# Non-weight transfers issued by GpSimd in a hybrid decoder kernel, with a changed table chain

## The chip, the cores and the metric

One core of one Trainium2 chip. The time is device microseconds of one execution of the program, the median of the runs shown. Engines are called as in the profile: PE (TensorE), DVE (VectorE), ACT (ScalarE), POOL (GpSimd) and SP (SyncE, which here only issues transfers).

## The reference, cut to what matters

Two layers of a decoder trunk, on 512 prompt tokens and 8 sample tokens together (520 columns), width 1024, FFN width 2816, all in fp32.

```python
def decoder_layer(x, ...):
    h = rms_norm(x, norm_g[0])
    x = x + 0.5 * rms_norm(swiglu(h, ...ffn 0), norm_g[1])
    h = rms_norm(x, norm_g[2])
    xq, xf, xi, xg, gu, gv, su, gate_cols = split(h @ w_in)
    a_out, s_hg_new = hgrn2_mixer(xq, xf, xi, xg, s_hg, lb, hgrn_norm_g)
    b_out, v_rows = gmlp_mixer(gu, gv, ...)
    c_out, h_re_new, h_im_new = s5_mixer(su, h_re, h_im, lam, log_dt, b, c, d, glu_w, glu_b)
    merged = sum(sigmoid(gates) * (branches @ w_branch))
    x = x + rms_norm(merged @ w_out, norm_g[3])
    h = rms_norm(x, norm_g[4])
    return x + 0.5 * rms_norm(swiglu(h, ...ffn 1), norm_g[5]), states
```

The S5 mixer is a complex diagonal recurrence, with `abar = exp(lam * dt)` and input and output matrices built from powers of abar. The kernel builds those matrices itself, as 16 tables (8 per layer).

## The kernel before, in words

Columns are held in two halves of 256 and 264. Every product is made of three matmuls (`mm3`: L122 weight high part by activation high part, L123 weight low part by activation high part, L125 weight high part by activation low part). A weight tile of 128x1024 is loaded by SP into `raw` (L102), ACT makes the high part `whi` (L103), DVE subtracts and makes the low part `wlo` (L107); with `share` the subtraction is done by POOL instead, in `ptt` (L237). `share` is asked for in two pairs of the first part of an FFN and in `ffn_units`, 25 tiles in all.

An FFN runs in three parts (`FF_PARTS`: 7, 7, 8 blocks of 128). Each part has up products (two matmul groups, `scaled` into `va` and `vb` on DVE, L129, silu on ACT, product on DVE, L416, then the split into `hid`, L115 on ACT and L116) and then down products over 8 output blocks.

Side work is cut into generators and advanced by `tick(us)`: each tick adds us over the step's price to a counter, and the generator goes on by one yield for each whole unit. `s5_tables` is such a generator in the first FFN, with the price `STEP_P`. It loads constants, computes the HGRN lower bounds (L516 to L531), then the S5 parameters (`s5_params`, from L569: dt = e^log_dt at L582 on POOL, xr = lam_r * dt at L585 on DVE, powers, sines and cosines, complex products in `cmul`, L504 to L509), and then the 16 tables (`s5_table`). A table takes POOL 19 instructions: `er` and `ei` (L665 to L667), `tb` 3 (L683 to L688), `cmul` for the next `bar` and a memset of `tb` 2 (L674). PE multiplies `er` and `ei` by `rc` (L695) into `tb` 0 and, through ACT copies (L704) and DVE (L709), into `tb` 2. Then four stores put `tb` 0 to 3 into memory (L711). `er` and `ei` exist once, so those of the next table can only be written when L695 has read the last ones. The FFN's last part begins after `before_last`, which drains what is left of the generator.

In the mixer, the S5 scan is another such generator, next to the HGRN heads and the gMLP. Its input is turned over through memory: `ud` and `us` are stored (L771, L772) and loaded back as `ub`, which lies in the `y` tiles (L777, L779). For each of 8 steps it loads four tables (L795), PE projects (L803), POOL saves and replaces columns of `w` (L827 to L830), DVE scans, and PE multiplies by the tables (L857 to L859). Every second step's result goes through memory once more (`zd`, L867 and L870).

At a block boundary (`residual`) x is updated, its high part `h` is made by ACT (`pre_hi`), its low part by DVE (`pre_lo`), squares are summed, and `norm_rows` has PE reduce the sum (`mean_w`, L257). DVE makes the inverse root there (`rs_s`, L225 to L233) and a diagonal matrix (`diag`, L268 and L272), and PE spreads it over the partitions (L279). The first norm of the program sums the squares one tile at a time (`sq_sum`, L218).

All 920 transfers are issued by SP, in program order, and each waits there for its data and its room. Every engine runs its own instructions in a fixed order.

Of the kernel before, what the change touches and what calls it, by code (L numbers as in the profile page):

```python
# [9 lines left out]
F32 = mybir.dt.float32  # L10
# [23 lines left out]
STEP_P, STEP_S, STEP_H = 3.9, 2.0, 3.1  # L34
# [11 lines left out]
class Trunk:  # L46
# [29 lines left out]
    def load_consts(self):  # L76
        nc, t, c = self.nc, self.t, self.const
        self.mask = c.tile([P, 64 + 3 * SEGS * 32], U8, name="mask")
        with self.tc.tile_pool(name="mkp", bufs=1) as pool:
            m = pool.tile([P, 64 + 3 * SEGS * 32], F32, name="m")  # L80
            nc.sync.dma_start(m, t["level_mask"])
            nc.gpsimd.tensor_copy(self.mask, m)
        self.tri = c.tile([P, P], F32, name="tri")
        nc.sync.dma_start(self.tri, t["tri_mask"])
        self.hg = c.tile([P, DEPTH * 4], F32, name="hg")
        nc.sync.dma_start(self.hg, t["hgrn_norm_g"])
        self.glub = c.tile([P, DEPTH * 8], F32, name="glub")
        nc.sync.dma_start(self.glub, t["glu_b"])
# [6 lines left out]
    def unit(self, src, *shape, pool=None, share=False):  # L95

        nc = self.nc
        n = math.prod(shape)
        raw = self.wp.tile([P, 1024], F32, tag="raw", name="raw", bufs=RAW_BUFS)
        hi = (pool or self.wp).tile([P, 1024], F32R, tag="whi", name="whi")  # L100
        lo = (pool or self.wp).tile([P, 1024], F32R, tag="wlo", name="wlo")
        nc.sync.dma_start(raw[:, :n], src)  # L102
        nc.scalar.copy(hi[:, :n], raw[:, :n])  # L103
        if share:
            self.ptt(lo[:, :n], raw[:, :n], hi[:, :n].bitcast(F32), ALU.subtract)
        else:
            nc.vector.tensor_tensor(lo[:, :n], raw[:, :n], hi[:, :n].bitcast(F32), ALU.subtract)  # L107
        pat = {2: "p (a b) -> p a b", 3: "p (a b c) -> p a b c"}[len(shape)]
        kw = dict(zip("abc", shape))
        return hi[:, :n].rearrange(pat, **kw), lo[:, :n].rearrange(pat, **kw)  # L110
# [232 lines left out]
    def residual(self, half, r1, y2, x2, pre, spill):  # L343
        nc, v, sl, w = self.nc, self.nc.vector, SL[half], HW[half]
        if pre is not None and half == 0:
            self.new_h()
        acc = self.acc2_room()[:, :, :w] if pre is not None else None
        for q in range(KD // 2):
            t, xs = y2[q][:, :, sl], x2[q][:, :, sl]
            v.tensor_tensor(t, t, r1[:, None].to_broadcast([P, 2, w]), ALU.mult)  # L350
            v.tensor_tensor(xs, t, xs, ALU.add)
            for e in range(2):
                j = 2 * q + e
                if pre is None:
                    nc.sync.dma_start(self.t["y"][j][:, sl], xs[:, e])
                    continue
                self.pre_hi(*pre, half, j)
                if spill is not None:
                    nc.sync.dma_start(spill[j][:, sl], xs[:, e])
            if pre is not None:  # L360
                yield
        if pre is None:
            return
        for q in range(KD // 2):
            xs = x2[q][:, :, sl]
            self.pre_lo(*pre, half, 2 * q)
            self.pre_lo(*pre, half, 2 * q + 1)
            if q == 0:
                nc.scalar.activation(acc, xs, AF.Square)
                continue  # L370
            t = y2[q][:, :, sl]
            nc.scalar.activation(t, xs, AF.Square)
            if q == 1:
                v.scalar_tensor_tensor(acc, t, 4e-6, acc, ALU.add, ALU.add)
            else:
                v.tensor_tensor(acc, acc, t, ALU.add)
            if q == 1:
                yield
        self.h_done[half] = True
        yield  # L380
        v.tensor_tensor(acc[:, 0], acc[:, 0], acc[:, 1], ALU.add)
        self.norm_rows(acc[:, 0], half)

    def sq_sum(self, acc, xs):

        for j, x in enumerate(xs):
            self.sq_acc(acc, x, j)
# [10 lines left out]
    def ffn(self, l, f, hid_pool, gain, finish, lo_eng=None, first=(), before_last=None, ahead=()):  # L398
# [3 lines left out]
        for part, nk in enumerate(FF_PARTS):  # L402
            hid = [hid_pool.tile([P, 2, NT], F32R, tag="hid", name="hid") for _ in range(nk)]

            def up(mi, half, u):
                (gh, gl), (uh, ul) = u
                pg, pu = self.pst(half), self.pst(half)
                xs = self.hx(half)
                self.mm3(pg, [(gh[:, k], gl[:, k]) for k in range(KD)], xs)
                self.passed()  # L410
                self.mm3(pu, [(uh[:, k], ul[:, k]) for k in range(KD)], xs)
                a, b, s = self.tmph("va", half), self.tmph("vb", half), self.tmph("sil", half)
                self.scaled(a, pg, half)
                nc.scalar.activation(s, a, AF.Silu)  # L414
                self.scaled(b, pu, half)
                nc.vector.tensor_tensor(b, b, s, ALU.mult)  # L416
                self.split(hid[mi][:, :, SL[half]], b, lo_eng)
                if m0 + mi >= 2:
                    self.tick(5.2)

            def pair(m, pool=None):
                share = part == 0 and LEAD <= m < LEAD + 2
                return [self.take(lambda: self.unit(t["w_up"][l, f, m0 + m, :, k], 8, 128, pool=pool, share=share))
                        for k in range(2)]
# [86 lines left out]
    def lower_bounds(self):  # L511

        nc, c = self.nc, self.const
        with self.tc.tile_pool(name="lbp", bufs=1) as pool:
            z = pool.tile([P, DEPTH, 4], F32, name="lb_z")
            nc.sync.dma_start(z, self.t["lb_logits"])  # L516
# [16 lines left out]
    def s5_tables(self, pool):  # L533
# [13 lines left out]
        def load(i):  # L547
            bc = pool.tile([P, 4, 2, 32], F32, tag="bc", name="bc", bufs=3)
            nc.sync.dma_start(bc, self.t["s5_bc"][i // 8, i % 8])
            return bc  # L550
# [18 lines left out]
    def s5_params(self, pool, NPR, k):  # L569
# [5 lines left out]
        nc.sync.dma_start(lr, t["lam_re"])  # L575
        nc.sync.dma_start(li, t["lam_im"])
        nc.sync.dma_start(ld, t["log_dt"])
        nc.sync.dma_start(k["d"], t["s5_d"])
# [27 lines left out]
        for i in range(3):  # L606
            self.cmul(pool, ar, ai, fr[:, :, i], fi[:, :, i], fr[:, :, i + 1], fi[:, :, i + 1], [NPR], v, "cs")
        v.memset(er[:, :, 3], 1.0)
# [32 lines left out]
    def s5_table(self, pool, l, s, k, rc, bc):  # L641
# [68 lines left out]
        for i in range(4):  # L710
            nc.sync.dma_start(dst[i], tb[i])  # L711
# [11 lines left out]
    def proj_block(self, l, m, evac, share=False):  # L723
        self.pu = self.unit(self.t["w_in"][l, m], 8, 128, share=share)
        for half in (0, 1):
            self.proj(l, m, half, lambda p: evac(half, p))
        self.tick(5.3)
# [4 lines left out]
    def ffn_units(self, l, f):  # L732
        return [lambda i=i: self.unit(self.t["w_up"][l, f, i // 2, :, i % 2], 8, 128, share=i % 2 == 0) for i in range(5)]

    def s5_project(self, l, f_block, ev_f):
# [32 lines left out]
        for m in range(4):  # L768
            d = self.dr.tile([P, 4, NT // 4], F32, tag="ud", name="ud", bufs=4)
            ds = self.dr.tile([P, NS], F32, tag="us", name="us", bufs=4)  # L770
            nc.sync.dma_start(d, ups[m])  # L771
            nc.sync.dma_start(ds, uss[m])  # L772
# [3 lines left out]
            for j in range(4):  # L776
                nc.sync.dma_start(ub[32 * j:32 * j + 32, :, :128], dv[j][:, :, :128])  # L777
            for j, c in ((3, 128), (0, 136)):
                nc.sync.dma_start(ub[32 * j:32 * j + 32, :, c:c + NS], ds.rearrange("(q c) n -> c q n", q=4))  # L779

    def s5_scan(self, l, pool):
# [5 lines left out]
        nc.sync.dma_start(st, t["state_s5"][l])  # L787
# [4 lines left out]
        def table(i, s, bufs=1):  # L792
            x = self.tab[l * n + s][i]
            tb = pool.tile([int(d) for d in x.shape], F32, tag=f"tab{i}", name="tab", bufs=bufs)
            nc.sync.dma_start(tb, x)  # L795
# [18 lines left out]
        for s in range(n):  # L814
# [50 lines left out]
            if lp == 2:  # L865
                d = self.dr.tile([P, 4 * NB], F32, tag="zd", name="zd", bufs=4)
                nc.sync.dma_start(d, zb.rearrange("p q n -> p (q n)"))  # L867
                dv = d.rearrange("(j c) (q n) -> q c j n", j=4, q=4)
                for k in range(4):
                    nc.sync.dma_start(zz[32 * k:32 * k + 32], dv[k])  # L870
# [18 lines left out]
        nc.sync.dma_start(t["s5_sample"][l], new)  # L889
        nc.sync.dma_start(t["s5_prompt"][l], fin)  # L890
# [55 lines left out]
    def tok_proj(self, name, l, c, evac, share=False):  # L946

        nc = self.nc
        us = [self.unit(self.t[name][l, c, kk], 4, 256, share=share) for kk in range(2)]
# [34 lines left out]
    def hgrn_values(self, l, hh, pool, V):  # L984
# [13 lines left out]
        nc.sync.dma_start(vd, vs)  # L998
# [36 lines left out]
    def hgrn_head(self, l, h, V, q0, qs, k, f, sg, pool, last):  # L1035
# [80 lines left out]
        def load(b0):  # L1116
            st = pool.tile([P, 2, P], F32, tag="st", name="st", bufs=2)
            nc.sync.dma_start(st, t["state_hgrn"][l, h][:, b0:b0 + 2])
            vb = pool.tile([P, 2, P], F32, tag="vb", name="vb", bufs=2)
            for b in range(2):  # L1120
                nc.sync.dma_start(vb[:, b], vd[b0 + b].partition_broadcast(P))
            loaded.append((st, vb))

        def state(b0):
# [4 lines left out]
            nc.sync.dma_start(t["hgrn_sample"][l, h][:, b0:b0 + 2], st)  # L1129
# [56 lines left out]
        nc.sync.dma_start(t["hgrn_prompt"][l, h], S[3])  # L1186
# [41 lines left out]
    def gmlp_norm(self, l, pool):  # L1228
# [3 lines left out]
        nc.sync.dma_start(ng, t["gmlp_ng"][l])  # L1232
        nc.sync.dma_start(nb, t["gmlp_nb"][l])
# [18 lines left out]
        nc.sync.dma_start(t["gmlp_v"][l], vt[4][:NS])  # L1252

    def gmlp_mix(self, l, pool, fill):
# [4 lines left out]
        nc.sync.dma_start(ws, t["gmlp_ws"][l])  # L1259
        bs = pool.tile([P, 4, P], F32, name="bs")  # L1260
        nc.sync.dma_start(bs, t["gmlp_bs"][l])
        w00 = pool.tile([NS, 4], F32, name="w00")
        nc.sync.dma_start(w00, t["gmlp_w00"][l])
# [31 lines left out]
    def mixer(self, l, xd, finish, ahead):  # L1295
# [46 lines left out]
        with tc.tile_pool(name=f"mh{l}", bufs=KD) as mh:  # L1342
# [4 lines left out]
            for j in range(KD):  # L1347
                nc.sync.dma_start(self.x[j], xd[j])
# [17 lines left out]
    def run(self, ctx):  # L1366
# [7 lines left out]
        def start(half):  # L1374
# [3 lines left out]
            self.sq_sum(accs[half], [self.x[j][:, SL[half]] for j in range(KD)])  # L1378
# [144 lines left out]
```

## Time and profile before

| | us |
|---|---|
| median of 3 runs (2705.0 to 2705.9) | 2705.61 |
| the profiled execution | 2704.64 |
| its span, first to last instruction | 2702.8 |
| PE busy | 2640.5 (98%) |
| DVE busy | 1597.4 (59%) |
| ACT busy | 1062.8 (39%) |
| POOL busy | 573.1 (21%) |

The span lies within the profiled execution; 1.8 us are around it. Mean granted clock of PE over the span is 0.993. Issuing a transfer doesn't count as busy, on any engine. Waits are given as the idle time of an engine ahead of an instruction, with the instruction that ended it last.

### The profile page before, as it was taken

What the parts mean: (1) busy time and instruction counts of PE and PEld (TensorE: products, weight loads), DVE (VectorE), ACT (ScalarE), POOL (GpSimd) and SP (SyncE); (2) the same over time, 40 slices, a digit from 0 to 9 for tenths busy, and PEclk for the clock granted to TensorE, in tenths of its full rate; (3) what the DMA queues carried; (4) which work ended last, traced back from release to release, by engine and by line L of the source; (5) the groups of instructions that cost most, each with busy time, mean ns of one, the idle gap of its engine ahead of it and who ended that gap; (6) DMA issues with size and microseconds to landing.
All of it is one profiled execution on the core that took longest, in us unless ns stands there. A gap on an engine that the chain in (4) does not pass through costs nothing.

```text
span 2702.8 us, 53557 instructions
## 1 busy us (share of the span) xinstructions
PE 2640.5 (98%) x21600; PEld 2615.5 (97%) x21600; DVE 1597.4 (59%) x3421; ACT 1062.8 (39%) x2166; POOL 573.1 (21%) x772
## 2 busy tenths in 40 slices
PE   8899999999999999999999999999999999999998
PEld 7899999999999999999999999998999999999998
DVE  8567877886675473344473344679866545534444
ACT  4244454453333453322443323544434335433232
POOL 5478920220021122011121101012100111201010
PEclk9999999999999999999999999999999999999999
DMA  4344453553232413322322232355332233232331
GB/s 140 102 137 150 151 159 113 171 159 96 88 95 87 141 56 95 97 91 95 94 79 87 93 96 89 123 152 169 116 99 90 89 107 111 69 98 88 99 94 48
DMA packets 131704, 291.22 MB, mean 108 GB/s; under 512 B 19024, under 2 KB 59632, under 8 KB 131456
## 3 DMA queue, kind: packets, MB, share of 16 engines
q1 hardware_dynamic: 131456, 287.79, 33.5%
q8 instruction: 170, 2.79, 0.4%
q14 instruction: 78, 0.64, 0.1%
HBM read 257.07 MB, written 30.67 MB: 106 GB/s over the span
## 4 chain that ended last, share of the span: by engine, by line
PE 80%; issue 7%; DVE 6%; POOL 4%; DMA 2%; ACT 1%; SPq 0%; DVEq 0%; POOLq 0%; ACTq 0%
PE mm L122 24%; PE mm L125 24%; PE mm L123 24%; PE mm L956 1%; PE mm L958 1%; PE mm L957 1%; DMA raw<-in_w_in 1%; PE aux L1073 1%; PE aux L279 1%; PE aux L257 1%; PE aux L695 0%; DVE h L317 0%; DVE acc L218 0%; PE aux L803 0%; DMA x<-in_xT 0%
## 5 line engine op out<-in xcount | busy, mean ns | idle before, releaser
L122 PE MATMUL mm<-h,whi 128*128 128x256 f32 (+1 forms) x4224 | 1059.0, 287 | 22.5 <-ACT h L313 7.0
L123 PE MATMUL mm<-h,wlo 128*128 128x256 f32 (+1 forms) x4224 | 1047.8, 284 | 1.9 <-DVE wlo L107 1.9
L122 PEld LDWEIGHTS mm<-h,whi 128*128 128x128 f32 x4224 | 799.8, 189 | 25.5 <-issue 8.2
L123 PEld LDWEIGHTS mm<-h,wlo 128*128 128x128 f32 x4224 | 802.2, 190 | 3.8 <-DVE wlo L107 3.0
L103 ACT CAST whi<-raw 128x1024 fp32r<-128x1024 f32 (+1 forms) x424 | 437.5, 1032 | 515.6 <-PE mm L125 431.4
L107 DVE TENSOR_TENSOR wlo<-raw,whi 128x1024 fp32r<-128x1024 f32 (+1 forms) x399 | 486.7, 1220 | 243.8 <-ACT whi L103 240.1
L125 PE MATMUL mm<-h,whi 128*128 128x256 f32 (+1 forms) x4224 | 596.9, 284 | 0.0
L125 PEld LDWEIGHTS mm<-h,whi 128*128 128x128 f32 x4224 | 544.4, 189 | 0.1
L122 PE MATMUL mm<-hid,whi 128*128 128x256 f32 (+1 forms) x1408 | 349.6, 285 | 3.6 <-ACT hid L115 3.6
L123 PE MATMUL mm<-hid,wlo 128*128 128x256 f32 (+1 forms) x1408 | 347.8, 283 | 0.0
L116 POOL TENSOR_TENSOR hid<-vb,hid 128x256 fp32r<-128x256 f32 (+1 forms) x132 | 132.5, 1004 | 871.8 <-ACT hid L115 858.9
L129 DVE TENSOR_TENSOR va<-mm,r 128x256 f32<-128x256 f32 (+1 forms) x320 | 136.0, 425 | 279.9 <-PE mm L125 274.9
L122 PEld LDWEIGHTS mm<-hid,whi 128*128 128x128 f32 x1408 | 265.8, 189 | 3.9 <-ACT hid L115 3.8
L123 PEld LDWEIGHTS mm<-hid,wlo 128*128 128x128 f32 x1408 | 266.3, 189 | 0.1
L125 PE MATMUL mm<-hid,whi 128*128 128x256 f32 (+1 forms) x1408 | 201.0, 283 | 0.0
L129 DVE TENSOR_TENSOR vb<-mm,r 128x256 f32<-128x256 f32 (+1 forms) x176 | 74.9, 425 | 188.6 <-PE mm L125 188.5
L125 PEld LDWEIGHTS mm<-hid,whi 128*128 128x128 f32 x1408 | 183.0, 189 | 0.0
L115 ACT CAST hid<-vb 128x256 fp32r<-128x256 f32 (+1 forms) x176 | 72.1, 410 | 277.5 <-DVE vb L416 274.2
L414 ACT ACTIVATE sil<-va 128x256 f32<-128x256 f32 (+1 forms) x176 | 73.7, 419 | 148.0 <-DVE va L129 142.1
L447 DVE TENSOR_TENSOR y<-mm,y 128x264 f32<-128x264 f32 (+1 forms) x128 | 54.3, 426 | 112.9 <-PE mm L125 112.3
L416 DVE TENSOR_TENSOR vb<-vb,sil 128x256 f32<-128x256 f32 (+1 forms) x176 | 84.1, 478 | 16.5 <-ACT sil L414 2.5
L958 PE MATMUL mm<-whi,h 128*128 128x256 f32 (+1 forms) x320 | 90.5, 283 | 0.0
(445 smaller groups left out, 3600.5 us busy)
## 6 DMA issues: line engine op xcount, KB each, us to landing
raw<-in_w_up SPq DMA_DIRECT2D x176, 512.0 KB, 3.6
raw<-in_w_in SPq DMA_DIRECT2D x88, 512.0 KB, 3.6
raw<-in_w_down SPq DMA_DIRECT2D x64, 448.0 KB, 3.3
raw<-in_w_down SPq DMA_DIRECT2D x32, 512.0 KB, 3.4
tab<-tb SPq DMA_DIRECT2D x48, 256.0 KB, 2.4
tab<-tab SPq DMA_DIRECT2D x48, 256.0 KB, 2.9
raw<-in_w_branch SPq DMA_DIRECT2D x24, 512.0 KB, 4.0
raw<-in_w_out SPq DMA_DIRECT2D x16, 512.0 KB, 4.0
```

The lines of the kernel that those rows point to most:

```text
L103: nc.scalar.copy(hi[:, :n], raw[:, :n])
L107: nc.vector.tensor_tensor(lo[:, :n], raw[:, :n], hi[:, :n].bitcast(F32), ALU.subtract)
L115: nc.scalar.copy(pair[:, 0], src)
L116: (lo_eng or nc.gpsimd).tensor_tensor(pair[:, 1], src, pair[:, 0].bitcast(F32), ALU.subtract)
L122: mm(out, wh, x[:, 0], start=first and k == 0, stop=False)
L123: mm(out, wl, x[:, 0], start=False, stop=False)
L125: mm(out, wh, x[:, 1], start=False, stop=last and k == n - 1)
L129: self.nc.vector.tensor_tensor(dst, p, self.rms(half), ALU.mult)
L414: nc.scalar.activation(s, a, AF.Silu)
L416: nc.vector.tensor_tensor(b, b, s, ALU.mult)
L447: nc.vector.tensor_tensor(ys, pd, ys, ALU.add)
L958: nc.tensor.matmul(p, self.h[k][:, 1, tk], wh, start=False, stop=k == KD - 1)
```

## The change

Four parts.

1. Every transfer but weights, the x input, norm_g and the result y is issued by GpSimd (`nc.gpsimd.dma_start` for `nc.sync.dma_start`). SP keeps 457 transfers, POOL gets 463. Among them, over the program: table stores 64, table loads 64, `vb` 64, `st` 32, hgrn states out 32, `ub` 48, `zz` 32, `xd` stores 32 and loads 16, `bc` 16, `ud`, `us` and `zd` 8 each.
2. `share` is gone: DVE makes every `wlo`.
3. In `residual` the squares and their sums move into the loop behind `pre_hi`, and all `pre_lo` come behind; `norm_rows` follows without a yield of its own. `sq_sum` takes two tiles at a time.
4. `STEP_P` 3.9 becomes 3.2, the generator is ticked in the first FFN's up blocks from the fifth on rather than the third, and `s5_params` has a yield more in a loop of three complex products.

```diff
-STEP_P, STEP_S, STEP_H = 3.9, 2.0, 3.1
+STEP_P, STEP_S, STEP_H = 3.2, 2.0, 3.1
...
-        if share:
-            self.ptt(lo[:, :n], raw[:, :n], hi[:, :n].bitcast(F32), ALU.subtract)
-        else:
-            nc.vector.tensor_tensor(lo[:, :n], raw[:, :n], hi[:, :n].bitcast(F32), ALU.subtract)
+        nc.vector.tensor_tensor(lo[:, :n], raw[:, :n], hi[:, :n].bitcast(F32), ALU.subtract)
...
                 if spill is not None:
-                    nc.sync.dma_start(spill[j][:, sl], xs[:, e])
-            if pre is not None:
-                yield
+                    nc.gpsimd.dma_start(spill[j][:, sl], xs[:, e])
+            if pre is None:
+                continue
+            nc.scalar.activation(acc if q == 0 else t, xs, AF.Square)
+            if q == 1:
+                v.scalar_tensor_tensor(acc, t, 4e-6, acc, ALU.add, ALU.add)
+            elif q:
+                v.tensor_tensor(acc, acc, t, ALU.add)
+            yield
         if pre is None:
             return
...
+        v.tensor_tensor(acc[:, 0], acc[:, 0], acc[:, 1], ALU.add)
+        for j in range(KD):
+            self.pre_lo(*pre, half, j)
+            if j == 3:
                 yield
         self.h_done[half] = True
-        yield
-        v.tensor_tensor(acc[:, 0], acc[:, 0], acc[:, 1], ALU.add)
         self.norm_rows(acc[:, 0], half)
...
-    def sq_sum(self, acc, xs):
-
-        for j, x in enumerate(xs):
-            self.sq_acc(acc, x, j)
+    def sq_sum(self, acc, half):
+
+        nc, w = self.nc, HW[half]
+        a2 = self.acc2_room()[:, :, :w]
+        for q in range(KD // 2):
+            xs = self.x2[q][:, :, SL[half]]
+            if q == 0:
+                nc.scalar.activation(a2, xs, AF.Square)
+                continue
+            sq = self.twos(self.yp, "y", 2, 576)[0][:, :, :w]
+            nc.scalar.activation(sq, xs, AF.Square)
...
+        nc.vector.tensor_tensor(acc[:, :w], a2[:, 0], a2[:, 1], ALU.add)
...
-                if m0 + mi >= 2:
+                if m0 + mi >= 4:
                     self.tick(5.2)
...
             self.cmul(pool, ar, ai, fr[:, :, i], fi[:, :, i], fr[:, :, i + 1], fi[:, :, i + 1], [NPR], v, "cs")
+            yield
...
         for i in range(4):
-            nc.sync.dma_start(dst[i], tb[i])
+            nc.gpsimd.dma_start(dst[i], tb[i])
...
             for j in range(4):
-                nc.sync.dma_start(ub[32 * j:32 * j + 32, :, :128], dv[j][:, :, :128])
+                nc.gpsimd.dma_start(ub[32 * j:32 * j + 32, :, :128], dv[j][:, :, :128])
```

The other transfers change in the same way. Of the instructions' order, three places.

**SP, from the first FFN's first part to its second.** Before, where `tab` is a table's place in memory and `raw` a weight tile:

```order
L102 DMA raw<-in_w_up 128x1024 x6
L549 DMA bc<-in_s_bc 128x256
L711 DMA tab_0_1_1641<-tb_1658 128x512
L711 DMA tab_0_3_1643<-tb_1660 128x512
L102 DMA raw<-in_w_down 128x896 x8
L102 DMA raw<-in_w_up 128x1024 x5
```

With the change:

```order
L102 DMA raw<-in_w_up 128x1024 x12
L102 DMA raw<-in_w_down 128x896 x8
L102 DMA raw<-in_w_up 128x1024 x14
L102 DMA raw<-in_w_down 128x896 x8
L102 DMA raw<-in_w_up 128x1024 x16
L102 DMA raw<-in_w_down 128x1024 x8
```

The two table stores that stood ahead of the eight w_down loads are gone from SP, as is the load of `bc`.

**POOL, in the middle of the tables**, where `er` and `ei` of the next table are made. Before:

```order
L665 TENSOR_TENSOR tt_3838<-bar,er 128x256
L666 TENSOR_TENSOR tt_3839<-bar,ei 128x256
L674 MEMSET tb_3651 128x256
L667 TENSOR_TENSOR er<-tt_3838,tt_3839 128x256
L665 TENSOR_TENSOR tt_3838<-bar,ei 128x256
L666 TENSOR_TENSOR tt_3839<-bar,er 128x256
L667 TENSOR_TENSOR ei<-tt_3838,tt_3839 128x256
```

With the change (`tab_4_1` is a store of the table before):

```order
L668 TENSOR_TENSOR tt_4420<-bar,er 128x256
L669 TENSOR_TENSOR tt_4421<-bar,ei 128x256
L551 DMA bc<-in_s_bc 128x256
L714 DMA tab_4_1_4189<-tb_4206 128x512
L677 MEMSET tb_4207 128x256
L670 TENSOR_TENSOR er<-tt_4420,tt_4421 128x256
L668 TENSOR_TENSOR tt_4420<-bar,ei 128x256
L669 TENSOR_TENSOR tt_4421<-bar,er 128x256
L670 TENSOR_TENSOR ei<-tt_4420,tt_4421 128x256
L510 TENSOR_TENSOR bar<-cm 128x64
L511 TENSOR_TENSOR bar<-cm 128x64
L714 DMA tab_4_0_4188<-tb_4205 128x512
```

POOL issues `bc` and stores between its own instructions; over a whole table there are four stores and one `bc`.

**POOL, at the start of the first S5 scan**, the second half of the transfers that turn over its input, and the first work on `w`; an x4 stands for four transfers, `y` is here the room of `ub`:

```order
L774 DMA ud<-up 128x520
L775 DMA us<-up 128x8
L774 DMA ud<-up 128x520
L775 DMA us<-up 128x8
L798 DMA tab<-tab_1_0_2044 128x512
L780 DMA y<-ud 32x4x128 x4
L782 DMA y<-us 32x4x8 x2
L780 DMA y<-ud 32x4x128 x4
L782 DMA y<-us 32x4x8 x2
L830 COPY s_new<-w 128x2x16
L831 MEMSET w 128x4
L833 COPY w<-s_h_6576 128x4x8
```

The same eight rows without `tab` (16 transfers: `ud`, `us`, `ud`, `us` and four rows of `y`) stand ahead of this piece, so that 33 transfers come between the first `ud` and the first work on `w`. Before, POOL has none here: its copies on `w` (L827, L830) follow memsets and other copies directly. PE's first matmul on `w` stands 100 matmuls behind the scan's first matmul now.

## Rows read from the trace of the kernel before

**Rows 1.** The page: busy time, share of the span and instructions of each engine.
```profile
PE 2640.5 (98%) x21600; PEld 2615.5 (97%) x21600; DVE 1597.4 (59%) x3421; ACT 1062.8 (39%) x2166; POOL 573.1 (21%) x772
```

**Rows 2.** Waits of PE: engine, line, waited for, us in all, times, longest us.
```profile
PE mm L122 <- DVE va L129: 6.9, 3, 3.1
PE aux L279 <- DVE diag L272: 6.2, 4, 2.4
PE mm L122 <- DVE vb L129: 4.8, 1, 4.8
...
PE mm L122 <- ACT hid L115: 3.6, 1, 3.6
...
PE mm L122 <- DVE rs_s L232: 3.0, 1, 3.0
```

**Rows 3.** Windows: length, busy (records) of PE, PEld, DVE, ACT, POOL; granted clock, DMA share, GB/s.
```profile
42.00:67.00 25.00, 25.00 (x211) 25.00 (x210) 24.76 (x57) 5.78 (x9) 17.95 (x22) 1.00 0.19 65
71.25:78.05 6.80, 5.59 (x26) 5.62 (x27) 6.80 (x19) 0.83 (x2) 6.80 (x17) 0.50 0.25 75
105.40:108.80 3.40, 3.40 (x18) 3.40 (x17) 2.81 (x6) 2.62 (x5) 0.00 (x0) 0.50 0.31 102
```

**Rows 4.** Timeline of POOL and DVE near 27 us: start, duration, instruction, idle before.
```profile
28.31 5.43 POOL L582 TENSOR_TENSOR dt<-ebase,log_dt 128x32 f32<-128x32 f32 x1
...
33.77 0.19 DVE L585 TENSOR_TENSOR xr<-lam_r,dt 128x32 f32<-128x32 f32 x1 [3.69 <-POOL dt L582]
```

**Rows 5.** Timeline, 45 to 51 us: weight splits on POOL, and DVE work beside them.
```profile
44.92 7.48 POOL L237 TENSOR_TENSOR wlo<-raw,whi 128x1024 fp32r<-128x1024 f32 x3
...
47.52 2.62 DVE L416 TENSOR_TENSOR vb<-vb,sil 128x264 f32<-128x264 f32 x1
...
57.29 0.41 DVE L487 SCALAR_TENSOR_TENSOR y<-y 128x256 f32<-128x256 f32 x1
...
L107 DVE TENSOR_TENSOR wlo<-raw,whi x399: 1076/1225/1755, 6.6 to 2643.3; 128x1024 fp32r<-128x1024 f32 x168, 128x896 fp32r<-128x896 f32 x32
```

**Rows 6.** Timeline of SP and ACT, 81 to 102 us.
```profile
81.45 15.07 SPq L711 DMA_DIRECT2D tab<-tb  x2
...
101.64 0.94 ACT L103 CAST whi<-raw 128x896 fp32r<-128x896 f32 x1 [11.09 <-DMA raw<-in_w_down]
```

**Rows 7.** Windows of POOL alone, about one table each: length, busy (records), clock, DMA, GB/s.
```profile
344.20:356.80 12.60, 10.46 (x13) 1.00 0.45 154
sum 77.00, POOL 69.42; mean POOL 11.57
```

**Rows 8.** Timeline of POOL in one table, 276 to 283 us.
```profile
276.88 0.74 POOL L667 TENSOR_TENSOR er<-tt,tt 128x256 f32<-128x256 f32 x1
...
278.32 0.61 POOL L666 TENSOR_TENSOR tt<-bar,er 128x256 f32<-128x256 f32 x1
279.00 0.74 POOL L667 TENSOR_TENSOR ei<-tt,tt 128x256 f32<-128x256 f32 x1
...
282.50 1.72 POOL L685 TENSOR_TENSOR tb<-tt,tt 128x256 f32<-128x256 f32 x1
```

**Rows 9.** Timelines of SP, POOL and PE at the start of the first S5 scan.
```profile
466.26 0.33 SPq L771 DMA_DIRECT2D ud<-up  x1
...
467.66 0.44 SPq L772 DMA_DIRECT2D us<-up  x1
471.17 1.75 SPq L777 DMA_DIRECT2D y<-ud  x4
...
477.65 0.67 POOL L827 COPY s_new<-w 128x32 f32<-128x32 f32 x1
...
478.93 0.10 POOL L828 MEMSET w<- 128x4 f32 x1
...
475.64 1.14 PE L803 MATMUL aux<-y,tab 128*128 128x144 f32 x8
```

**Rows 10.** The page: a group of POOL, mean ns of one behind its busy time.
```profile
L116 POOL TENSOR_TENSOR hid<-vb,hid 128x256 fp32r<-128x256 f32 (+1 forms) x132 | 132.5, 1004 | 871.8 <-ACT hid L115 858.9
```

## What the change will do to the time

> **What bounds the kernel now.** I read the busy line first: TensorE (PE) is busy 2640.5 of 2702.8 us [rows 1], so a change can win only what PE still waits and what it loses at half clock, and can lose as much as it makes PE wait. In undisturbed work 211 matmuls took 25.00 us [rows 3], 0.1185 us each; that is PE's pace below. The profiled execution took 2704.64 us, 1.0 us under the median of 2705.61; the sum is made against the former, and the median is taken to move by as much.
>
> Next the waits of PE [rows 2]. Each has a place. (A) 3.0 us for rs_s, the first norm's chain on DVE. (B) 4.8 us for vb at 67 us. (C) 3.1 us for va at 101 us, the longest of three. (D) 3.6 us for hid at 246 us. (E) The diag waits at the block boundaries, 6.2 us in four. The windows behind B and C show the granted clock at 0.50, the lower of its two levels (1.2 of 2.4 GHz), for 6.8 and 3.4 us [rows 3]. PE had waited just before in both; half of such a stretch, 3.4 and 1.7 us, is lost too.
>
> Then the engines behind these waits. For A: DVE stood 3.69 us at xr, in its fixed order ahead of the norm chain, until POOL had done dt, a power of 5.43 us [rows 4]. For B: DVE was busy 24.76 of the 25.00 us before it [rows 3], and beside a weight split on POOL a DVE operation took 2.62 us where one of about this size took 0.41 later [rows 5]. For C: SP stood 15.07 us over two table stores whose tile POOL and ACT had not finished, the w_down loads stood behind them, and ACT waited 11.09 us for its weights [rows 6]. Last POOL itself, in the stretch where it makes the 16 S5 tables (140 to 360 us): 10.46 us busy in its quietest window of 12.60 us, and 69.42 in 77.00 us over six [rows 7]. It is the next engine to be full.
>
> **The change, part by part.**
>
> 1. *Issue moves from SP to POOL.* 463 DMAs now take POOL's time in program order. No row shows an issue on POOL. From below it is bounded by SP's issue of the same transfer, 0.33 us [rows 9]; from above by a POOL instruction that works on a tile while other engines are active, 1004 ns on the mean [rows 10]. I take 0.6 us, which is what POOL's commonest instruction on one 128x256 tile takes with nobody in its way, 0.61 us [rows 8], and keep both ends.
>
> 2. *What SP gains.* Only weights, x, norm_g and the result stay on SP, so nothing stands ahead of the w_down loads. C goes: -3.1 and -1.7, **-4.8 us**. The store that waits for its tile now stands in POOL's order, just behind the work that makes er and ei; its tile hangs on matmuls that POOL has waited for anyway, so I add no wait for it.
>
> 3. *The table chain.* A table on POOL becomes its compute, 10.46 us [rows 7], and five issues (four stores, one bc load): 10.46 + 5 x 0.6 = 13.46 us. The new order puts the first table matmul of the 16 tables at 1066 and the last at 2470 of the listed matmuls (before: 913 and 2566), so PE comes by for 15 tables within 1404 x 0.1185 = 166.4 us, 11.1 us each. Each needs er and ei, which exist once. POOL writes them in 276.88 to 279.74, 2.9 us [rows 8], so it may fall behind by 11.1 - 2.9 = 8.2 us before PE stands. 15 x 13.46 = 201.9 us, less 166.4 and 8.2: **+27.3 us**, in steps of about two us on most tables. Lost clock isn't added, since PE waits for POOL there at either clock. With 0.33 us the same sum gives 181.7 - 174.6 = +7.1; with 1.0, 231.9 - 174.6 = +57.3.
>
> The Trainium skill, "SBUF — State Buffer", section "Who interferes with whom" and its trap on DVE and DMAs from GpSimd, says that GpSimd cannot write the descriptors of its DMAs while DVE runs a two-port operation, and gives 620 ns for a transfer alone against 3100 ns beside such an operation. By that, five issues would cost an estimated 3.1 to 15.5 us per table; no run yet shows such an issue. It is the third rival.
>
> 4. *The S5 scan.* After the first ud store at 466.26 us, POOL now has 33 DMAs before the copies and memsets that finish the first w: 33 x 0.6 = 19.8 us. The wait for ud to land and come back, 468.10 to 471.17, moves to POOL too: 3.1 us [rows 9]. The copies and memsets took 477.65 to 479.03, 1.4 us [rows 9]. So w is ready at 490.6. PE's first matmul on w is now 100 matmuls behind the scan's first at 475.64, at 487.5 us. That is 3.1 us late, once in each layer: **+6.2 us**. With 0.33 us it is ready at 481.7 and nothing is lost; with 1.0 at 503.8, 16.3 us per layer.
>
> 5. *Weight splits back on DVE.* Four splits in the first FFN at 1.22 us each [rows 5] cost DVE 4.9 us and free it of the slowed operations, 2.2 us each in [rows 5]; later splits have weights in reserve and cost nothing while TensorE's queue of weights is ahead. Together with the chain that starts later and in smaller pieces, B shrinks. It is 4.8 + 3.4 = 8.2 us, but DVE has the same work to do in that stretch; I take half, **-4 us** (bounds 0 and -8.2).
>
> 6. *First norm.* dt now stands before lb_e on POOL, and POOL asks for its input itself near the start of the program, where SP asked for it behind weight loads. A goes: **-3 us** (bounds 0 and -3.0). Against that, mask and table inputs now compete with the first weights and x: **+1 us** (0 to 3, the latter A's size).
>
> 7. *Boundaries.* Squares are taken inside the loop, and the statistic's matmuls come 17 to 35 matmuls earlier in PE's order, some 2 to 4 us. An earlier matmul gains only if DVE delivers earlier. Of E's 6.2 us I take a third, **-2 us** (bounds +2 and -6.2). D hangs on the last tables and stays: 0 (bound -3.6).
>
> Sum: -4.8 + 27.3 + 6.2 - 4 - 3 + 1 - 2 = +20.7 us; on the median, **2726 us**.
>
> **The rivals.**
>
> *POOL keeps up, and the kernel is faster.* If an issue costs POOL what it costs SP, 0.33 us, the chain loses 7.1 us and the scan nothing: -4.8 + 7.1 - 4 - 3 + 1 - 2 = -5.7; with D and the rest of B gone as well, -13.5. About **2696 us**. It decides at the issue price where 15 tables fit into 174.6 us, that is 11.6 us a table, 0.24 us per issue, for no loss in the chain, and at about 0.4 us for the whole. For it: POOL is only 21% busy overall [rows 1], and SP's price is the one row of the same kind of instruction. Against it: the window at 10.46 of 12.60 us [rows 7].
>
> *Break-even.* Prices of 0.35 to 0.47 us bring gains and losses within 0.2% of each other, 5.4 us, which is about what a measurement of this kernel tells from no change. About **2706 us**.
>
> *Issue on POOL is dear.* DVE is nearly always at work beside the tables, and the same POOL instruction on a 128x256 tile takes 0.74 us or, beside DVE, 1.72 [rows 8]. If issues are drawn out likewise, to 1.0 us, the chain costs 57.3 and the scans 32.6: -4.8 + 57.3 + 32.6 - 4 - 3 + 1 - 2 = +77.1, **2783 us**. For it: POOL and DVE visibly hold each other up [rows 5, 8]. Against it: the quiet windows.
>
> **How the numbers follow.** Forecast 0.45, POOL keeps up 0.34, break-even 0.09, dear 0.12. The price of an issue decides, and 0.6 us lies nearest to the plain POOL rows. Hence slower 0.57, same 0.09, faster 0.34. The range runs from 2689 (POOL keeps up, B and D gone, and three us of clock behind D) to 2778, just short of the dear case, which leaves out about 2 in 10. The forecast's own range, with issues of 0.5 to 0.8 us, is 2713 to 2755.
>
> **What the profile will show.** Right: PE waits at the table matmuls for POOL's er and ei, two us at a time, between 150 and 380 us; POOL without gaps there; C's wait gone and ACT's wait for w_down with it; a wait for w or s_new early in both scans. POOL's gaps between its compute instructions give the price of an issue directly. Wrong: table matmuls without waits, with POOL gaps of 0.4 us or less per DMA; or PE waiting in the scan far more than in the tables, which would mean that the round trips through memory, and not the issues, fill POOL. If A or B stay while SP is free, DVE's own work and not its waits made them.

## The result

The changed kernel takes 2737.43 us (median of 4 runs, 2735.64 to 2744.19) against 2705.31 us of the kernel before in the same session: a ratio of 1.0125, 95% interval 1.0106 to 1.0143, 32 us slower. The forecast was 2726 us, slower, with a range of 2689 to 2778.

The page of the changed kernel, busy time of each engine, and the two queues that carry data:

```profile
PE 2654.1 (97%) x21600; PEld 2625.8 (96%) x21600; DVE 1631.8 (60%) x3440; ACT 1060.5 (39%) x2158; POOL 746.1 (27%) x1210
...
q1 hardware_dynamic: 65808, 222.44, 25.4%
q0 software_dynamic: 23760, 65.35, 7.9%
```

Against [rows 1], PE works 14 us more, at half clock (its mean granted clock is 0.988, against 0.993), and the span is 34 us longer. POOL has 1210 instructions: the 772 of before less 25 splits plus 463 transfers, so an issue on POOL counts as busy. That issuing doesn't count as busy on any engine, as the section on time and profile before has it, holds for SP and not for POOL. 65 MB now go through POOL's queue.

PE's waits, the view that answers to [rows 2]:

```profile
PE aux L698 <- DVE k L703: 7.5, 1, 7.5
PE aux L698 <- POOL ei L670: 7.3, 5, 2.0
PE aux L861 <- DVE w L850: 7.1, 5, 1.6
PE mm L119 <- DVE va L126: 5.9, 4, 2.0
PE mm L119 <- DVE vb L126: 4.1, 2, 2.1
...
PE aux L806 <- DMA tab<-tab: 3.2, 2, 1.7
...
PE mm L119 <- ACT hid L112: 2.8, 2, 2.5
...
PE aux L806 <- DMA y<-us: 2.8, 2, 2.1
PE aux L276 <- DVE diag L269: 2.4, 1, 2.4
...
PE aux L698 <- POOL er L670: 1.4, 2, 0.8
```

The waits for rs_s (A), of 4.8 us for vb (B) and of 3.1 us for va (C) are gone. In their place stand waits at the table matmuls (L698: k, ei, er, 16.2 us), and in the scans (L806 and L861, on w and on transfers). Where the time went can be read from PE alone: the 20160 matmuls of the products come in the same order in all kernels, so the start time of number n can be compared. Differences to before, in us, of the profiled executions; each column is a stretch between two such numbers, and what stands behind the last product (0.5 us in the changed kernel) is in none:

| | to 400: start, first norm, parameters | 400 to 1300 | 1300 to 3200: tables | 3200 to 4200: scan 1 | 13500 to 14200: scan 2 | block boundaries | the rest |
|---|---|---|---|---|---|---|---|
| forecast | -6 | -4.8 | +27.3 | +3.1 | +3.1 | -2 | 0 |
| changed kernel | -8.3 | -4.3 | +39.7 | +12.6 | +8.5 | -10.8 | -3.8 |
| moves undone | -9.2 | -4.7 | +14.7 | +1.2 | -0.4 | -10.9 | -2.2 |
| moves alone | -2.4 | +3.0 | +24.9 | +12.3 | +7.4 | +1.5 | -2.4 |
| tables on SP | -11.2 | -5.8 | +14.4 | +9.4 | +5.6 | -10.9 | -2.3 |
| scan on SP | -10.4 | -4.5 | +38.1 | +7.8 | +11.6 | -10.8 | -3.9 |
| moves undone, 3.9 | -8.6 | -6.5 | +15.6 | +0.9 | +0.9 | -10.9 | -2.2 |
| HGRN on SP | -10.5 | -7.2 | +38.4 | +5.3 | +6.6 | -10.9 | -3.8 |
| stores halved | -10.2 | -7.2 | +53.7 | +6.1 | +5.8 | -10.8 | -2.6 |
| splits on POOL | -6.2 | +1.0 | +14.3 | +1.0 | +0.8 | +10.6 | -2.2 |
| no splits alone | -5.7 | -5.3 | -0.1 | +0.4 | +2.9 | -11.0 | -3.6 |
| old chain | -3.7 | -5.5 | +2.1 | +0.9 | +1.2 | -10.5 | -1.6 |
| constants on POOL | -10.9 | -5.5 | +1.7 | +1.4 | +1.4 | -10.9 | -2.2 |
| two edits | -9.6 | -4.7 | -0.6 | +0.3 | +0.1 | -10.9 | -2.2 |

In the tables, POOL's own line of work from one store of `tb` 3 to the next, one table's time (211 to 228 us):

```profile
211.23 0.56 POOL L714 DMA_DIRECT2D tab<-tb  x1 [0.30 <-POOL tb L691]
...
213.31 0.58 POOL L551 DMA_DIRECT2D bc<-in_s_bc  x1
...
214.14 0.54 POOL L714 DMA_DIRECT2D tab<-tb  x1
214.69 0.75 POOL L670 TENSOR_TENSOR er<-tt,tt 128x256 f32<-128x256 f32 x1
...
216.97 0.80 POOL L669 TENSOR_TENSOR tt<-bar,er 128x256 f32<-128x256 f32 x1
219.61 0.59 POOL L714 DMA_DIRECT2D tab<-tb  x1 [1.84 <-ACT k L702]
220.22 0.74 POOL L670 TENSOR_TENSOR ei<-tt,tt 128x256 f32<-128x256 f32 x1
...
226.35 0.59 POOL L714 DMA_DIRECT2D tab<-tb  x1
...
228.01 0.56 POOL L714 DMA_DIRECT2D tab<-tb  x1 [0.30 <-POOL tb L691]
```

From one `tab` store to its like 16.78 us pass. The five issues take 0.54 to 0.59 us each, 2.9 us. The store of `tb` 0 stands between the two halves of making `ei` and waited 1.84 us there for ACT's copies. In the next table such a store, at 236.24 us, waited 1.83 us, and PE then stood for the `ei` behind it:

```profile
237.63 0.90 PE L698 MATMUL aux<-rc,ei 128*128 128x160 f32 x2 [1.28 <-POOL ei L670]
```

Over all 64 stores (least, median, most):

```profile
L714 POOL DMA_DIRECT2D tab<-tb x64: 539/584/591, 87.3 to 387.7; - x64
```

A store's issue costs 0.58 us at the median and never more than 0.59, though DVE was at work beside 59 of the 64.

### The profile page after: what moved, and what is told of

It reads as the page before. It is cut to its first block, busy times and chain, and to the rows that moved or that the text cites. A ratio compares the mean times of both kernels' runs of the same rounds, so it can differ in the third digit from the quotient of the medians.

```text
span 2737.0 us, 53556 instructions
## 1 busy us (share of the span) xinstructions
PE 2654.1 (97%) x21600; PEld 2625.8 (96%) x21600; DVE 1631.8 (60%) x3440; ACT 1060.5 (39%) x2158; POOL 746.1 (27%) x1210
## 4 chain that ended last, share of the span: by engine, by line
PE 75%; POOL 8%; DVE 6%; issue 6%; DMA 3%; ACT 1%; SPq 0%; DVEq 0%; POOLq 0%; ACTq 0%
PE mm L119 23%; PE mm L122 23%; PE mm L120 23%; PE aux L1076 1%; DVE wlo L104 1%; POOL tab L714 1%; PE mm L959 1%; PE mm L960 1%; PE mm L961 1%; POOL tt L669 1%; POOL tt L668 1%; PE aux L276 1%; DMA raw<-in_w_in 1%; PE aux L254 1%; DMA y<-zd 0%
## 5 line engine op out<-in xcount | busy, mean ns | idle before, releaser
L104 DVE TENSOR_TENSOR wlo<-raw,whi 128x1024 fp32r<-128x1024 f32 (+1 forms) x424 | 520.2, 1227 | 247.0 <-ACT whi L103 243.7
L960 PE MATMUL mm<-wlo,h 128*128 128x256 f32 (+1 forms) x320 | 90.9, 284 | 0.0
```

The source lines that it names most:

```text
L960: nc.tensor.matmul(p, self.h[k][:, 0, tk], wl, start=False, stop=False)
```

## The experiments

**The first four.** Undo the moves; make the moves alone; and put two groups of transfers back on SP.

*Moves undone*:

```diff
-        nc.gpsimd.dma_start(vd, vs)
+        nc.sync.dma_start(vd, vs)
...
```

and so for all 463.

> The changed kernel with all 463 transfers back on SP; splits, boundaries, first norm and table pace as changed. Theory (POOL's issues make the loss): the table stretch loses its 41 us and the two scans their 13 and 8 us, the boundaries keep their gain of about 10 us, and SP stands over table stores again (C, about 5 us): 2690 to 2700 us. Rival (the table chain's closer pace, 1404 matmuls for 16 tables against 1653, fills POOL and DVE by itself): the table stretch keeps more than half of its loss, 2715 us or more.

2693.18 us against 2704.37, ratio 0.9966 (0.9953 to 0.9979). The theory holds for the sum, the rival for part of the table stretch: 14.7 of its 39.7 us stay without any issue on POOL. PE's largest wait at the tables is still there:

```profile
225.79 0.60 PE L698 MATMUL aux<-rc,er 128*128 128x160 f32 x1 [6.43 <-DVE k L703]
```

```profile
221.30:231.50 10.20, 5.71 (x25) 5.74 (x26) 7.26 (x17) 6.13 (x20) 8.04 (x14) 0.50 0.43 155
```

It is the seventh table's first matmul. The closer chain puts tables six and seven 52 matmuls, some 6 us, apart (1566 and 1618 of the listed matmuls), where the old one had 148 between them, and a table needs more than twice that: POOL ended its last instruction for `tb` 3 (L691) at 199.4, 214.0 and 228.2 us. With the half clock behind it (the second row, a window: busy times of PE, PEld, DVE, ACT and POOL, then the clock; 0.50 from within the wait until 5.7 us behind it, so 2.9 lost), this one place is 9.3 of the 14.7 us. In the changed kernel it is the wait of 7.5 us for k.

*Moves alone*: the kernel before with the same 34 lines of code issuing from GpSimd and nothing else.

> The kernel before with only the 463 transfers moved to GpSimd; splits, boundaries, first norm and the pace of 1653 matmuls for 16 tables as before. Theory (issues on POOL of 0.57 us each): 2.9 us more per table at a pace of 13.1 us where POOL was busy 10.5 to 12.8, so 5 to 20 us there, the scans lose about 20 us, waits A and C go (8 us): 2720 to 2740 us. Rival (the closer pace makes the table loss): nothing lost in the tables, 2710 to 2720 us.

2751.38 us against 2704.37, ratio 1.0169 (1.0147 to 1.0190), slower than both statements had it. The tables lose 24.9 us, which with the 14.7 of the pace makes the 39.7 of the changed kernel: the two losses add up. The scans lose 19.7. PE still waits 5.8 us for vb at 70 us (B). C is gone: with SP free, ACT no longer waits for w_down weights there. But PE waits 6.0 us for va at 92 us, for another reason. A weight split on DVE, begun while POOL issued a table store, took 9.52 us, where such splits take 1.2; it ended about 1.1 us after POOL first paused, for 0.30 us ahead of its next store:

```profile
81.54 0.57 POOL L711 DMA_DIRECT2D tab<-tb  x1
...
90.54 0.59 POOL L711 DMA_DIRECT2D tab<-tb  x1 [0.30 <-POOL tb L688]
```

```profile
81.81 9.52 DVE L107 TENSOR_TENSOR wlo<-raw,whi 128x1024 fp32r<-128x1024 f32 x1
```

```profile
92.57 0.55 PE L122 MATMUL mm<-h,whi 128*128 128x256 f32 x1 [6.02 <-DVE va L129]
```

Two DVE operations of 5.5 us stand beside such stores at 251 and 269 us, and the changed kernel has one of 5.79 us at 268 us. Where the tables' transfers are on SP and no split is on POOL (moves undone, tables on SP, no splits alone), no DVE operation took as much as 2 us. So the issues seem to cost DVE time too; why, no run shows.

*Tables on SP*: four stores and the `bc` load of each table.

```diff
-            nc.gpsimd.dma_start(bc, self.t["s5_bc"][i // 8, i % 8])
+            nc.sync.dma_start(bc, self.t["s5_bc"][i // 8, i % 8])
...
-            nc.gpsimd.dma_start(dst[i], tb[i])
+            nc.sync.dma_start(dst[i], tb[i])
```

> The changed kernel with the 64 table stores and 16 bc loads back on SP, all else as changed. Theory: POOL's table falls from 16.8 us to about 11.8, the table stretch loses most of its 41 us, some 5 us come back as the C wait; 2695 to 2710 us. Rival (the pace, or DVE, bounds the stretch): 2725 us or more.

2707.45 us, ratio 1.0010 (1.0000 to 1.0020), in the theory's range. The table stretch falls to 14.4 us, the same as with all moves undone: the 80 issues, with the waits that they bring, are the whole of the other 25 us. No C wait came back.

*Scan on SP*: `ud`, `us`, `ub`, the table loads, `zd`, its way back and the load of the S5 state.

> The changed kernel with the S5 scan's transfers (ud, us, ub, tables, zd and its way back, the state) on SP, all else as changed. Theory (POOL's queue of issues in the scan): the scan stretches lose their 13 and 8 us, 2714 to 2720 us. Rival (the scan's loss comes from the other order of the matmuls and the HGRN transfers on POOL): 2728 us or more.

2731.08 us, ratio 1.0102 (1.0087 to 1.0117): the rival's range. In this profile 19.4 us of the scans' 21.1 stay, with HGRN's transfers and a few others (the gMLP's, the S5 states out) left on POOL. Rows of POOL there, 626 to 635 us:

```profile
626.49 0.54 POOL L1121 DMA_DIRECT2D st<-in_state_hgrn  x1 [2.76 <-PE aux L1139]
632.13 0.54 POOL L1132 DMA_DIRECT2D out_hgrn_sample<-st  x1 [5.10 <-DVE st L1131]
632.66 0.53 POOL L1124 DMA_DIRECT2D vb<-vd  x1
633.21 1.66 POOL L234 TENSOR_TENSOR TT<-f 128x256 f32<-128x256 f32 x1
```

In the kernel before, the last of these had no transfer ahead of it:

```profile
602.65 0.73 POOL L237 TENSOR_TENSOR TT<-f 128x256 f32<-128x256 f32 x1 [6.43 <-ACT acc L1195]
```

A store of HGRN's state waits 5.10 us for DVE, a load of it 2.76 us for a PE matmul to free its room, and the running product `TT`, which the head needs, queues behind them. SP stood in these waits before, with nothing but other transfers behind it.

**The second four.**

*Moves undone, 3.9*: as moves undone, with one number more.

```diff
-STEP_P, STEP_S, STEP_H = 3.2, 2.0, 3.1
+STEP_P, STEP_S, STEP_H = 3.9, 2.0, 3.1
```

> The changed kernel with all transfers back on SP and STEP_P at 3.9 again (the tables over 1644 matmuls rather than 1404). Theory now (the table stretch lost in two ways: 25 us to issues on POOL, 14.6 us to a pace at which DVE and the ring of single buffers can't follow): the 14.6 us go too, 2676 to 2682 us. Rival (the 14.6 us come from something else in the later chain, such as running into the down products): 2690 us or more.

2693.07 us, ratio 0.9957 (0.9942 to 0.9972): the rival's range. Up to product 2500 the loss is down to 3.5 us, but a chain that starts late and goes slowly has its last table behind product 2784 (2400 with the closer pace) and costs 12.1 us behind 2500. This run alone doesn't tell its start from its pace; the run old chain, below, does.

*HGRN on SP*: `vd`, `st`, `vb` and the two state outputs back, S5 on GpSimd.

> The changed kernel with only the HGRN transfers (vd, st, vb, the two state outputs) back on SP; S5's stay on GpSimd. Theory (POOL's queue is full in the scan, and what stands behind HGRN transfers that wait for DVE comes late): the stretch from matmul 3500 to 4200 loses its 8 us and 13500 to 14200 its 8.5 us, the 4.6 us from 3200 to 3500 stay: 2718 to 2724 us. Rival (either group alone fills the queue, so taking one away gives nothing, as the S5 group gave only 5 us): 2732 us or more.

2723.57 us, ratio 1.0070 (1.0053 to 1.0087), in the theory's range, and its interval is clear of the changed kernel's (1.0106 to 1.0143), as that of scan on SP is not: of the two groups HGRN's is the one that is shown to cost time. What each costs can't be read from the table's columns. Three kernels with the same code in the scans (changed, tables on SP, stores halved) have 21.1, 15.0 and 11.9 us there, so the 11.9 us of this one, and the 19.4 us of scan on SP, lie within what profiles of one code differ by.

*Stores halved*:

```diff
-            nc.gpsimd.dma_start(dst[i], tb[i])
+            for z in range(2):
+                p = slice(64 * z, 64 * z + 64)
+                nc.gpsimd.dma_start(dst[i][p], tb[i][p])
```

> The changed kernel with each table store issued as two halves of 64 partitions: 64 issues more on POOL, the same bytes. Theory (POOL's time per issue sets the table stretch, 0.57 us each): 64 x 0.57 = 36 us more, 2765 to 2780 us. Rival (the stretch hangs on waits in POOL's order, for ACT's copies and for stores to land, and not on the time of issues): under 15 us more, below 2752 us.

2743.11 us, ratio 1.0143 (1.0127 to 1.0158): the rival's range. The price of an issue is as it was, with half the bytes and half the partitions:

```profile
198.17 1.10 POOL L716 DMA_DIRECT2D tab<-tb  x2
...
202.89 1.11 POOL L716 DMA_DIRECT2D tab<-tb  x2
...
209.88 1.56 POOL L716 DMA_DIRECT2D tab<-tb  x3
```

(0.52 to 0.56 us each.) 64 of them should cost 36 us by the theory; the table stretch loses 14.0 more. In this profile from the end of one table's issues at 211.4 us to the next's at 228.3 us it is 16.8 us, as it was with half the stores: the wait for ACT of 1.84 us has been filled with issues. That fits a ring (PE's table matmuls, ACT's copies, POOL's store and `ei`, PE again) that bounds the stretch, in which an issue costs only where it lies on it; no run tests the ring by itself. The scans, whose code is the same in both, differ by 9 us between these two profiles; I leave that open.

*Splits on POOL*: as moves undone, with `share` in its three places as before.

> The changed kernel with all transfers back on SP and the 25 weight splits on POOL again as before. Theory (the splits on POOL held DVE up in the first FFN, wait B): 4 to 8 us slower than with the transfers undone alone, 2697 to 2701 us, with B's wait at 60 to 70 us back. Rival (B went because the chain starts later and in finer steps): within 2 us of it, 2691 to 2695 us.

2724.94 us, ratio 1.0077 (1.0062 to 1.0092): 32 us slower than without the splits, more than either statement. To product 1300 they cost 8.8 us (waits at the places of B and C are back, 2.4 and 3.7 us), and at the boundaries 21.5: with the splits on POOL the new boundary code is 10.6 us slower than the old.

**The last four.**

*No splits alone*: the kernel before, with every split on DVE.

```diff
-                share = part == 0 and LEAD <= m < LEAD + 2
+                share = False
...
-        return [lambda i=i: self.unit(self.t["w_up"][l, f, i // 2, :, i % 2], 8, 128, share=i % 2 == 0) for i in range(5)]
+        return [lambda i=i: self.unit(self.t["w_up"][l, f, i // 2, :, i % 2], 8, 128) for i in range(5)]
```

> The kernel before with one edit: no weight split on POOL, all 25 on DVE. Theory (the splits on POOL hold DVE up at the boundaries as well as at wait B; boundaries in the new form gain nothing by themselves): 8 to 16 us faster than before, 2689 to 2697 us, with about 9 us of it at the three boundaries. Rival (the new order of squares and low parts makes the boundary gain): the boundaries stay as before, and only wait B shrinks: 2699 to 2705 us.

2681.55 us against 2705.10, ratio 0.9913 (0.9899 to 0.9927): the theory's way, but beyond its range. This one edit wins 23.6 us. B and C are gone from PE's waits, A and D stay:

```profile
PE mm L122 <- DVE va L129: 4.2, 3, 1.9
PE mm L122 <- ACT hid L115: 4.2, 2, 3.7
...
PE mm L122 <- DVE rs_s L232: 3.0, 1, 3.0
PE aux L279 <- DVE diag L272: 2.4, 1, 2.4
```

The boundaries gain 11.0 us with their old code; the new code gives 10.9 with the splits away, so it adds nothing to that. Why, is seen at the first boundary. The kernel before, POOL and DVE:

```profile
960.92 2.39 POOL L237 TENSOR_TENSOR wlo<-raw,whi 128x1024 fp32r<-128x1024 f32 x1 [22.59 <-ACT whi L103]
...
969.44 2.39 POOL L237 TENSOR_TENSOR wlo<-raw,whi 128x1024 fp32r<-128x1024 f32 x1 [6.13 <-ACT whi L103]
```

```profile
961.04 2.29 DVE L231 TENSOR_TENSOR rs_s<-col 128x2 f32<-128x2 f32 x1
...
970.05 2.08 DVE L218 TENSOR_TENSOR acc<-acc,sq 128x264 f32<-128x264 f32 x1
```

and without the splits, DVE:

```profile
948.48 0.16 DVE L231 TENSOR_TENSOR rs_s<-col 128x2 f32<-128x2 f32 x1
```

A step of the root on a 128x2 tile takes 2.29 us while POOL subtracts, and 0.16 without that. In all, 15 DVE operations took over 2 us in the kernel before, and none here. Such a step holds DVE's whole line, and PE waits for `diag` at the end of it. C goes too, but SP still stands 14 us at a table store there: with the splits on DVE the program's order has two w_down loads ahead of that store, and PE has weights meanwhile.

*Old chain*: as moves undone, with STEP_P 3.9 and the ticks from the third up block on.

> The changed kernel with all transfers back on SP, STEP_P 3.9 and the ticks from the third up block on: no splits on POOL, new boundaries and first norm, the chain at nearly its old places (1016 to 2708). Theory (the close pace costs 14.6 us; a late and slow chain runs into the down products instead): neither loss, 2678 to 2686 us, the best so far. Rival (the earlier chain brings waits B and C back): 2690 us or more.

2686.79 us, ratio 0.9932 (0.9919 to 0.9945), just above the theory's range. The tables lose 2.1 us, where moves undone, 3.9 lost 15.6 with the same pace and a later start: there it was the start. What is missing is a wait of PE of 4.3 us at the first norm, where DVE again stood at `xr` for POOL's `dt`:

```profile
35.29 0.19 DVE L587 TENSOR_TENSOR xr<-lam_r,dt 128x32 f32<-128x32 f32 x1 [4.41 <-POOL dt L584]
```

*Constants on POOL*: the same with nine transfers at the program's start (masks, HGRN and S5 parameters) on GpSimd.

> The same with the nine transfers of constants at the start (masks, HGRN bounds, S5 parameters) on GpSimd, where POOL has nothing else to do. Theory (issues on POOL cost only where POOL or its queue is full): 0 to 3 us faster than with all on SP. Rival (mask and constants then compete with the first weights and x): 1 to 2 us slower.

2679.65 us, ratio 0.9907 (0.9893 to 0.9921): 7.1 us faster than the run before, more than expected; the stretch to 400 gains 7.1 us. In old chain POOL had stood idle there for 18.6 us, and here PE's wait at the first norm is gone.

*Two edits*: the kernel before with no splits and these nine transfers on GpSimd.

> The kernel before with two edits: no weight split on POOL, and the nine constant transfers at the start on GpSimd (as in the run before, where they took away a wait of 4.4 us at the first norm and its half clock). Theory (the two gains are independent, and boundaries, first norm and chain in the new form add nothing): 4 to 6 us faster than no splits alone, 2675 to 2678 us. Rival (the new first norm is needed for the constants to help): 2680 to 2682 us.

2677.41 us against 2704.26, ratio 0.9902 (0.9885 to 0.9920): 27 us faster than before and 60 faster than the changed kernel, the lowest time of all, in the theory's range. Against the run before it the intervals overlap, so which of those two is faster is open. It keeps the old boundaries, first norm and chain. Against no splits alone the constants are worth 4.1 us here.

## Why the prediction was right, point by point

The direction, the main place of the loss and POOL's issues as one of its causes came as forecast; several sizes didn't, and that the time lies within the range owes something to luck.

- *The price of an issue* (step 1). Taken as 0.6 us, between 0.33 and 1.0. Measured: 0.58 at the median. The rival of cheap issues falls with it, and so does the dear one: no store took over 0.59 us. The rule of the Trainium skill ("SBUF — State Buffer", "Who interferes with whom") on issues drawn out beside DVE's two-port operations shows in none of these 64 rows: in five of them an fp32 copy on DVE had begun first and ran beside the issue (0.50 us from 280.91 us on, for one), and the issue kept its time; whether DVE took a two-port form there, no run here shows. What got long beside issues was DVE's work (moves alone).
- *The table chain* (step 3): +27.3 forecast, +39.7 measured. The issues, with the waits that they bring, are 25 us of it (tables on SP; moves alone). That this is near 27.3 is luck in part. The 10.46 us taken for POOL's own work come from a window with 13 of a table's 19 instructions [rows 7]; the table shown above has some 12 us of it (16.78 less 2.9 of issues, 1.84 and 0.30 of waits). "I add no wait for it" was wrong, by 1.84 us in each of five tables, and part of the issues fill such waits (stores halved). What failed is the even spacing, by which the closer pace costs nothing without issues: it has one gap of 52 matmuls, and the new chain costs 14.7 us with no issue on POOL at all, 9.3 of them at that gap, in a wait for DVE's `k` and not for POOL's `ei`.
- *The scans* (step 4): +6.2 forecast, +21.1 measured in this profile (15.0 and 11.9 in the two others with the same code there). The first 33 issues came as worked out (`ud` at 494.2, w complete at 515.5 us, 21.3 us against 24.3), but PE didn't stand at that `w`: its first wait there is one of 2.1 us for `us`. What the step left out is everything behind them: PE waits 5.4 us for tables that are loaded late and 7.1 us for DVE's `w` (the waits above), and stores and loads that wait for DVE or PE stand in POOL's line, HGRN's above all (HGRN on SP).
- *The splits* (step 5): -4 forecast for wait B. It went altogether. That later splits cost nothing failed: on POOL they held DVE up at every boundary, 11 us (no splits alone).
- *SP's relief* (step 2): -4.8 forecast and -4.3 measured in that stretch. C goes when only SP is relieved (moves alone), as forecast, though another wait comes there. It goes as well when the splits go, with all stores on SP (no splits alone), so in the changed kernel either would have done.
- *First norm* (step 6): A goes, as forecast, for 3 us; the start is later by 1.2 us against 1 forecast.
- *Boundaries* (step 7): -2 forecast for the new form; it gives nothing once the splits are gone, and loses 10.6 us while they stay (splits on POOL). The 10.8 us there belong to step 5.
- D stays, as forecast, at 2.5 us (3.6 before).

So the forecast was 13 us short by the traces: 27 us too little loss in tables and scans, 14 too little gain, mostly from the splits. Errors of both signs cancel in part. Of the signs named ahead, waits for `er` and `ei` of up to two us came, but PE's longest wait at the tables was for `k`, POOL had gaps there, and no early wait for the first `w` came.

## What to carry to other kernels

A transfer that is issued in an engine's own line brings its waits with it: before one moves it off a queue that does nothing else, look at what it waits for and at what then stands behind it, and move only those that wait for nothing (constants at the start gained 4 to 7 us, the rest lost 25 in the tables and 12 to 21 in the scans). When a change bundles several edits, take each alone; here one deletion held nearly all the gain, and the moves and the closer chain hid it. And a side chain's pace is better judged by its tightest gap than by its mean.

## What the runs showed of the hardware that was not expected

- The issue of a table store on POOL cost 0.52 to 0.59 us whether it moved 256 KB, half of that or less, and with DVE at work beside it.
- A DVE operation that began beside such an issue could last until POOL's next pause: 9.52 us in place of 1.2 in the worst case (moves alone). The cause is open.
- A subtraction on POOL with an fp32r result on 128x1024 took 2.4 us and could hold a DVE operation that overlaps with it for about its whole length: 2.29 us in place of 0.16. 25 splits that spared DVE 1.22 us each cost the kernel 24 us.
- PE's wait of 6.4 us for the seventh table cost 2.9 us more, because the granted clock fell to 0.50 during the wait and stayed there for 5.7 us of work behind it (moves undone, the window above).
